# Where the last three up projections stand in a layer's last feed-forward chunk

## The chip, the cores and the metric

The kernel runs on one core of a Trainium2 chip. TensorE (PE in the profile) multiplies matrices, VectorE (DVE) and ScalarE (ACT) do element-wise work, GpSimd (POOL) does a little of it, and SyncE (SP) issues nearly all DMA transfers. The metric is device time in microseconds (us), the median of several runs. The kernel before takes 2103.15 us: median of 3 runs, from 2100.36 to 2106.13.

## The reference

Two encoder layers work on 256 tokens of width 2048, in float32. Only the second half of a layer matters here; the first half (one input projection, two kinds of attention, one output projection) keeps its form.

```python
def depthwise_conv(u, w, bias):
    up = jnp.pad(u, ((0, 0), (1, 1), (0, 0)))
    return up[:, :-2] * w[0] + up[:, 1:-1] * w[1] + up[:, 2:] * w[2] + bias
...
        x = x + o @ w_out[l]
        h2 = rms_norm(x, ln2_g[l])
        u = depthwise_conv(h2 @ w_up[l], conv_w[l], conv_b[l])
        gate, up = u[..., :D_FF], u[..., D_FF:]
        x = x + (jax.nn.silu(gate) * up) @ w_down[l]
```

D_FF is 5632, so `w_up` is 2048 x 11264 and `w_down` 5632 x 2048 in each layer.

## The kernel before

**Two halves of a number.** A float32 operand is split into a high part (`whi`, written by ScalarE in L112) and the rest (`wlo`, written by VectorE in L113). TensorE multiplies high by high, low by high and high by low. All matmuls go through a helper in L98, so TensorE's work has that one line and is told apart by its tiles.

**Quanta and steps.** All weights are cut into pieces of 1 MB (128 x 2048). The list `quanta` holds them in the order of the program; a quantum is one such piece and the matmuls that use it. A step is half of a quantum, or a third of it for a quantum of the seven-product scheme. The main loop goes through the steps: `split_w` splits the weights of the step four ahead (`SPLIT_AHEAD`, five buffers each of `whi` and `wlo`), then come the matmuls of the step itself, then what the dictionary `side` has due there. When a quantum's last step is split, its `raw` buffer (three of them) is free and SP loads the quantum three ahead (`LOAD_AHEAD`, L733). Splits are traced with a priority of 40 instructions ahead of their place (`AHEAD_PRIO`). From this program a list scheduler makes a fixed order of instructions for each engine, by priority and by its own estimate of when each is ready; on the chip each engine runs its own list in order and waits where data are not there.

**Feed-forward.** The 5632 middle columns are 44 blocks of 128, called f. For each f there are two `up` quanta (`q_up`), which together accumulate gate and value in an `mm` tile of PSUM, and then `glu`: ScalarE and VectorE read the tile (L545, L546), VectorE multiplies by the normalising factor (L547), GpSimd copies a border, the convolution is one ScalarE and two VectorE operations for each half (L555, L557), then Silu, product (L561) and split, which gives `gs[f]`. For each pair of f whose products go through the seven-product scheme, `sums_mid` also makes four sums of blocks (L574 to L577).

The 44 blocks are cut into chunks of 8, 8, 8, 8 and 12 (`CHUNKS`). Output columns are four blocks nb of 512. Within a chunk:

- For the first 8 f (`PART`), output blocks 0 and 1 are computed by a scheme of seven products in place of eight, over pairs of f: four `seven` quanta (`q_seven`), each with three parts. Part 1 first has VectorE form sums of the weights in place (L739, 1024 columns, and L740 and L741, 512 each). Six sums stay open in PSUM from seven(0) to the end of seven(3): two halves of an `mm` tile, both `S` tiles, `tr` and `pv`. Then `add_seven` reads them (L617 to L625). What the scheme leaves out is one `plain` quantum (`q_plain`), for one sub-block, added in L654.
- Output blocks 2 and 3 are computed plainly, by `down` quanta (`q_down`, four f each): down(nb, g), g counting groups of four f. A finished block is added to x in L481.
- In the last chunk blocks 0 and 1 have one `down` quantum each, down(0,2) and down(1,2), for the four f outside of the scheme. down(0,2) takes an `mm` tile, down(1,2) `tr` and `pv`.

PSUM has two `mm` tiles in all. In the kernel before, `q_plain` takes one (`cur["dn"]`) and every later down(2, g) and down(3, g) of the chunk goes into it.

**Order in a chunk.** The first four chunks: ups to one f beyond the chunk, plain, then seven(i) and a down in turn. The last chunk: all ups to f = 43, plain, then as L706 to L722 say:

```python
quanta += [seven(0), down(2, 0), seven(1), down(2, 1), seven(2), down(2, 2), seven(3)]
quanta += [down(3, 0), down(0, 2), down(1, 2), down(3, 1), down(3, 2)]
```

**Leaving a layer.** When an output block is complete in the last chunk, `leave_x` (L694) puts its squares and transposes for the next layer (`square_x`, `turn_x`) at a quantum that comes some places later; the pair of numbers is (quanta later, half). In the last layer it stores the block instead, by DMAs on SP (L637). Two loads of the next layer's attention bias (L323) use the buffers in which the last products of `glu` lie.

Of the kernel before, what the change touches and what calls it, by code (L numbers as in the profile page):

```python
# [11 lines left out]
F32 = mybir.dt.float32  # L12
# [6 lines left out]
P = 128  # L19
L = 2  # L20
T = 256
TT = T // P
# [9 lines left out]
NF = FF // P  # L32
FG = 4


CHUNKS = (8, 8, 8, 8, 12)

PART = 8
PAIRS = PART // 2
# [20 lines left out]
def encoder_kernel(  # L60
# [10 lines left out]
    psum = ctx.enter_context(tc.tile_pool(name="psum", bufs=4, space=bass.MemoryType.PSUM))  # L71
# [333 lines left out]
    quanta = []  # L405
# [5 lines left out]
    def two(ps, w_h, w_l, mv, first, last):  # L411

        mm(ps, w_h, mv, first, False)
        mm(ps[:, 1], w_l, mv[:, 0], False, last)
# [12 lines left out]
    cur = {}  # L427
# [99 lines left out]
    def q_up(l, f, u):  # L527
        def body(q, half, hi, lo):
            if u == 0 and half == 0:
                cur["up"] = psum.tile([P, 2, 2, T], F32, name="mm", bufs=2)  # L530
            ps = cur["up"]
            hv, lv = (w.rearrange("p (k j n) -> p k j n", k=4, j=2) for w in (hi, lo))
            for j in range(2):
                for kk in range(4):
                    k = 8 * u + 4 * half + kk
                    two(ps[:, j], hv[:, kk, j], lv[:, kk, j], xs[k], k == 0, k == KD - 1)
            if u == 1 and half == 1:
                glu(l, f, ps)
        return body

    def glu(l, f, ps):
        ux = halo[f % 2]
        r = T // GRID_W
        t = work.tile([P, 2, T], F32, name="prob", bufs=2)
        nc.scalar.activation(t, ps[:, :, 0], AF.Copy)  # L545
        nc.vector.tensor_add(t, t, ps[:, :, 1])  # L546
        nc.vector.tensor_mul(ux[:, :, r:r + T], t, st["r2"][:, None, :].to_broadcast([P, 2, T]))  # L547

        nc.gpsimd.tensor_copy(ux[:, :, 1:r], ux[:, :, T:T + r - 1])  # L549
        nc.gpsimd.tensor_copy(ux[:, :, T + r:T + 2 * r - 1], ux[:, :, r + 1:2 * r])  # L550
        y = work.tile([P, 2, T], F32, name="pT", bufs=4)
        for j in range(2):
            c = j * NF + f
            w0, w1, w2, b = (par["conv"][:, l, i, c:c + 1] for i in range(4))
            nc.scalar.activation(y[:, j, :], ux[:, j, r:r + T], AF.Identity, scale=w1, bias=b)  # L555
            for w, o in ((w0, 0), (w2, 2 * r)):
                nc.vector.scalar_tensor_tensor(y[:, j, :], ux[:, j, o:o + T], w, y[:, j, :],  # L557
                                               op0=ALU.mult, op1=ALU.add)
        nc.scalar.activation(t[:, 0, :], y[:, 0, :], AF.Silu)  # L559
        m = work.tile([P, T], F32, name="bias", bufs=2)  # L560
        nc.vector.tensor_mul(m, t[:, 0, :], y[:, 1, :])  # L561
        gs[f] = middle(l, f)
        split(gs[f][:, 0], gs[f][:, 1], m)
        ms[f] = m
        if f % 2 and f < NF - CHUNKS[-1] + PART:
            sums_mid(l, f // 2, ms.pop(f - 1), ms.pop(f))
# [17 lines left out]
    def q_seven(l, c, i):  # L584

        f = sum(CHUNKS[:c]) + 2 * i
        p = f // 2
        a, b = slice(0, P), slice(P, T)

        def body(q, part, hi, lo):  # L590
            if i == 0 and part == 0:
                t = psum.tile([P, 2, 512], F32, name="mm", bufs=2)
                ps = {1: t[:, 0], 6: t[:, 1]}
                for n, name, k in ((5, "S", 2), (7, "S", 2), (3, "tr", 1), (4, "pv", 1)):
                    ps[n] = psum.tile([P, 512], F32, name=name, bufs=k)
                cur["seven"] = ps
            ps = cur["seven"]
            hv, lv = (w.rearrange("p (k n) -> p k n", k=2) for w in (hi, lo))
            todo = (((3, ss[p, 3]), (1, gs[f][:, :, a])),
                    ((7, ss[p, 2]), (5, ss[p, 0])),  # L600
                    ((4, gs[f + 1][:, :, b]), (6, ss[p, 1])))[part]
            for j, (n, x2) in enumerate(todo):
                for x_part, w in ((0, hv), (1, hv), (0, lv)):
                    mm(ps[n], x2[:, x_part], w[:, j], i == 0 and x_part == 0 and w is hv,
                       i == PAIRS - 1 and w is lv)
            if i == PAIRS - 1 and part == 2:
                with tc.high_priority(offset=AHEAD_PRIO):
                    add_seven(ps)
        return body
# [17 lines left out]
    def leave_x(q, l, nb, after):  # L627

        if l + 1 < L:
            at(q + after[0], square_x, nb, half=after[1])  # L630
            at(q + after[0], turn_x, l + 1, 0, nb, half=after[1])
            if nb == NB - 1:
                at(q + after[0], stat_x, 0)
        else:
            m = slice(nb * 512, (nb + 1) * 512)
            for tt in range(TT):
                nc.sync.dma_start(out=out[:, tt, m], in_=x[:, tt, m])  # L637
# [17 lines left out]
        return body  # L655

    def q_down(l, c, nb, g):
        f0, nf = sum(CHUNKS[:c]), CHUNKS[c]

        def body(q, half, hi, lo):  # L660
            if nb >= 2:
                ps = cur["dn"]
            elif half == 0:

                ps = cur["dn", nb] = (psum.tile([P, TT, 512], F32, name="mm", bufs=2) if nb == 0 else
                                      _Both(*(psum.tile([P, 512], F32, name=n, bufs=1) for n in ("tr", "pv"))))
            else:
                ps = cur["dn", nb]
            hv, lv = (w.rearrange("p (k n) -> p k n", k=2) for w in (hi, lo))
            i = FG * g + 2 * half  # L670

            last = l == L - 1 and c == len(CHUNKS) - 1 and nb == NB - 1
            cut = nf - FG if last or nb < 2 else 0
            if last and i >= cut:
                if i == cut:
                    add_x(nb, ps)
                    cur["end"] = [psum.tile([P, 512], F32, name="S", bufs=2) for _ in range(TT)]
                ps = _Both(*cur["end"])
            three(ps, (gs[f0 + i], gs[f0 + i + 1]), hv, lv, i in (0, cut), i in (cut - 2, nf - 2),
                  last and i == nf - 2)  # L680
            if i < nf - 2:
                return
            if last:
                for tt in range(TT):
                    xv = x[:, tt, nb * 512:(nb + 1) * 512]
                    nc.vector.tensor_add(xv, xv, ps[:, tt])  # L686
                    for j in range(2):
                        m = slice(nb * 512 + j * 256, nb * 512 + (j + 1) * 256)
                        (nc.sync, nc.scalar)[j].dma_start(out=out[:, tt, m], in_=x[:, tt, m])
                return  # L690
            with tc.high_priority(offset=4 * AHEAD_PRIO if c == len(CHUNKS) - 1 and nb == NB - 1 else 0):
                add_x(nb, ps)
            if c == len(CHUNKS) - 1:
                leave_x(q, l, nb, ((2, 0), (1, 1), (6, 0), (1, 1))[nb])  # L694
        return body

    for l in range(L):
        for j in range(NJ):
            for u in range(4):
                quanta.append((a["w_in"][l, j, u], q_win(l, j, u), ""))  # L700
        for grp in "ba":
            for nb in range(NB):
                for u in range(2):
                    quanta.append((a["w_out"][l, 0 if grp == "a" else 1, nb, u], q_wout(l, grp, nb, u), ""))
        f = 0
        for c, nf in enumerate(CHUNKS):  # L706

            end = min(sum(CHUNKS[:c + 1]) + 1, NF)
            while f < end:
                for u in range(2):  # L710
                    quanta.append((a["w_up"][l, f, u], q_up(l, f, u), "up"))
                f += 1
            down = lambda nb, g: (a["w_down"][l, sum(CHUNKS[:c]) // FG + g, nb], q_down(l, c, nb, g), "")
            seven = lambda i: (a["w_seven"][l, c, i], q_seven(l, c, i), "seven")
            quanta.append((a["w_plain"][l, c], q_plain(l, c), ""))
            if nf == 8:
                for i in range(4):
                    quanta += [seven(i), down(2 + i // 2, i % 2)]
            else:
                quanta += [seven(0), down(2, 0), seven(1), down(2, 1), seven(2), down(2, 2), seven(3)]  # L720
                quanta += [down(3, 0), down(0, 2), down(1, 2), down(3, 1), down(3, 2)]


    steps = [(q, h) for q in range(len(quanta)) for h in range(3 if quanta[q][2] == "seven" else 2)]
# [228 lines left out]
```

## Time and profile before

The profile is one execution, with a span (first to last instruction) of 2101.8 us. PE is TensorE matmuls, PEld its weight loads. "Granted clock" is the share of TensorE's full speed that the chip allowed.

| | |
|---|---|
| median of 3 runs | 2103.15 us (2100.36 to 2106.13) |
| the profiled execution's own time | 2103.54 us |
| its span | 2101.8 us |
| mean granted clock | 0.998 |
| TensorE matmuls busy | 2088.1 us |
| VectorE busy | 1724.5 us |
| ScalarE busy | 1221.6 us |
| read from HBM | 404.42 MB, 193 GB/s over the span |

A row of a timeline or of the chain begins with start and length in us. A number in square brackets is the idle time of the engine before the instruction, with what ended it. A row of waits gives the sum in us, the number of waits and the longest. A row of windows gives the stretch, its length, the busy time and count of each engine in turn (PE, PEld, DVE, ACT, POOL), then the granted clock, the share of busy DMA engines, and GB/s. A row of a group gives its count, busy time, mean ns of one, and the idle time before it. A row of loads gives count, size and us from issue to landing.

The last chunk of the first layer ends with its down quanta at about 1005 to 1046 us of the span, that of the second layer at the end of the span.

### The profile page before, as it was taken

The numbers are of one execution on the slowest core, as the hardware profiler recorded it, in microseconds if no ns is written. First come the engines' busy times: TensorE is split into PE (matmuls) and PEld (weight loads), VectorE is DVE, ScalarE is ACT, GpSimd is POOL, SyncE is SP. The second block draws the span as 40 slices with busy tenths as digits, with TensorE's granted clock in tenths as the row PEclk, the third lists the DMA queues.
The fourth block names the chain that finished last, engine by engine and source line by source line (L and its number), as shares of the span: only waits on it lengthen the run. The fifth ranks groups of instructions, "written<-read, shape, count | busy, mean of one in ns | idle before, by whom it ended". The sixth has DMA issues, their size and how long they took to land.

```text
span 2101.8 us, 29190 instructions
## 1 busy us (share of the span) xinstructions
PE 2088.1 (99%) x10816; PEld 1792.2 (85%) x10816; DVE 1724.5 (82%) x2604; ACT 1221.6 (58%) x1817; POOL 167.5 (8%) x237
## 2 busy tenths in 40 slices
PE   9999999999999999999999999999999999999998
PEld 8888888888888888888788888888888888888886
DVE  7786757898998989988857866678989989899886
ACT  7566656565655555556555665566555555565653
POOL 0011100100101001011000011001001010100110
PEclk9999999999999999999999999999999999999999
DMA  9544555556465565655555455555565656546554
GB/s 346 200 152 156 178 180 179 182 211 210 164 239 198 203 203 186 231 188 182 218 182 179 161 171 169 172 180 191 205 208 184 225 196 213 194 179 240 183 191 148
DMA packets 62145, 408.42 MB, mean 194 GB/s; under 512 B 7345, under 2 KB 9905, under 8 KB 13745
## 3 DMA queue, kind: packets, MB, share of 16 engines
q1 hardware_dynamic: 61280, 405.46, 55.9%
q8 instruction: 85, 1.39, 0.3%
q10 hardware_dynamic: 720, 1.08, 0.2%
q14 instruction: 60, 0.48, 0.1%
HBM read 404.42 MB, written 2.10 MB: 193 GB/s over the span
## 4 chain that ended last, share of the span: by engine, by line
PE 99%; DMA 1%; ACT 0%; DVE 0%; issue 0%; ACTq 0%; DVEq 0%
PE mm L98 89%; PE S L98 4%; PE pv L98 3%; PE tr L98 2%; PE tr L373 1%; DMA raw<-in_w_down 1%; PE tr L307 1%; PE S L149 0%; DVE wlo L113 0%; ACT whi L112 0%; ACT qtok L274 0%; ACT kT L315 0%; DVE x L686 0%; ACT tq L618 0%; DVE ones L90 0%
## 5 line engine op out<-in xcount | busy, mean ns | idle before, releaser
L112 ACT ACTIVATE whi<-raw 128x1024 fp32r<-128x1024 f32 (+1 forms) x797 | 829.9, 1057 | 696.9 <-PE mm L98 411.3
L113 DVE TENSOR_TENSOR wlo<-raw,whi 128x1024 fp32r<-128x1024 f32 (+1 forms) x797 | 963.7, 1220 | 278.9 <-ACT whi L112 238.3
L98 PE MATMUL mm<-xs,whi 128*128 128x512 f32 x2816 | 976.7, 390 | 0.0
L98 PE MATMUL mm<-xs,wlo 128*128 128x256 f32 x2816 | 794.1, 282 | 0.0
L98 PEld LDWEIGHTS mm<-xs,whi 128*128 128x128 f32 x2816 | 528.4, 188 | 110.4
L98 PEld LDWEIGHTS mm<-xs,wlo 128*128 128x128 f32 x2816 | 532.2, 189 | 0.9
L98 PE MATMUL mm<-whi,mid 128*128 128x512 f32 x1412 | 371.7, 394 | 7.1 <-ACT whi L112 7.1
L98 PEld LDWEIGHTS mm<-whi,mid 128*128 128x128 f32 x1412 | 265.2, 190 | 62.6 <-ACT whi L112 7.9
L98 PE MATMUL mm<-whi,xs 128*128 128x512 f32 x1152 | 294.3, 393 | 1.4 <-ACT qtok L274 1.3
L98 PEld LDWEIGHTS mm<-whi,xs 128*128 128x128 f32 x1152 | 213.1, 188 | 44.3 <-ACT qtok L274 1.8
L98 PE MATMUL mm<-wlo,mid 128*128 128x512 f32 x706 | 201.4, 392 | 0.0
L98 PE MATMUL mm<-wlo,xs 128*128 128x512 f32 x576 | 159.5, 393 | 0.0
L98 PEld LDWEIGHTS mm<-wlo,mid 128*128 128x128 f32 x706 | 132.1, 188 | 27.0
L557 DVE SCALAR_TENSOR_TENSOR pT<-halo,conv,pT 128x256 f32<-128x256 f32 x352 | 147.6, 478 | 0.9
L549 POOL COPY halo<-halo 128x6 f32<-128x6 f32 x88 | 34.3, 390 | 1199.6 <-DVE halo L547 1199.6
L98 PEld LDWEIGHTS mm<-wlo,xs 128*128 128x128 f32 x576 | 107.3, 188 | 21.6
L555 ACT ACTIVATE pT<-halo,conv 128x256 f32<-128x256 f32 x176 | 95.1, 587 | 5.8 <-DVE halo L547 5.7
L550 POOL COPY halo<-halo 128x6 f32<-128x6 f32 x88 | 79.4, 903 | 0.2 <-POOL halo L549 0.2
L547 DVE TENSOR_TENSOR halo<-prob,acc_b 128x512 f32<-128x512 f32 x88 | 60.6, 689 | 2.1
L546 DVE TENSOR_TENSOR prob<-prob,mm 128x512 f32<-128x512 f32 x88 | 59.8, 680 | 0.0
L559 ACT ACTIVATE prob<-pT 128x256 f32<-128x256 f32 x88 | 35.6, 404 | 35.0 <-DVE pT L557 35.0
L545 ACT ACTIVATE prob<-mm 128x512 f32<-128x512 f32 x88 | 51.4, 584 | 7.4 <-PE mm L98 7.4
(180 smaller groups left out, 1475.9 us busy)
## 6 DMA issues: line engine op xcount, KB each, us to landing
raw<-in_w_up SPq DMA_DIRECT2D x176, 1024.0 KB, 4.9
raw<-in_w_in SPq DMA_DIRECT2D x71, 1024.0 KB, 4.9
raw<-in_w_down SPq DMA_DIRECT2D x48, 1024.0 KB, 4.9
raw<-in_w_seven SPq DMA_DIRECT2D x40, 1024.0 KB, 5.0
raw<-in_w_out SPq DMA_DIRECT2D x32, 1024.0 KB, 4.9
raw<-in_w_plain SPq DMA_DIRECT2D x10, 1024.0 KB, 4.9
bias<-in_bias SPq DMA_DIRECT2D x16, 160.0 KB, 2.5
x<-in_x SPq DMA_DIRECT2D x4, 512.0 KB, 11.0
```

Source lines behind the costliest of these rows:

```text
L98: nc.tensor.matmul(ps, lhsT, rhs, start=start, stop=stop, skip_group_check=True)
L112: high = nc.scalar.activation(hi, src, AF.Copy)
L113: nc.vector.tensor_sub(lo, src, hi.bitcast(F32))
L307: nc.tensor.transpose(ps[:, j, tt * P:(tt + 1) * P], qn[tt][:, p + j, :], ident)
L545: nc.scalar.activation(t, ps[:, :, 0], AF.Copy)
L546: nc.vector.tensor_add(t, t, ps[:, :, 1])
L547: nc.vector.tensor_mul(ux[:, :, r:r + T], t, st["r2"][:, None, :].to_broadcast([P, 2, T]))
L549: nc.gpsimd.tensor_copy(ux[:, :, 1:r], ux[:, :, T:T + r - 1])
L550: nc.gpsimd.tensor_copy(ux[:, :, T + r:T + 2 * r - 1], ux[:, :, r + 1:2 * r])
L555: nc.scalar.activation(y[:, j, :], ux[:, j, r:r + T], AF.Identity, scale=w1, bias=b)
L557: nc.vector.scalar_tensor_tensor(y[:, j, :], ux[:, j, o:o + T], w, y[:, j, :], op0=ALU.mult, op1=ALU.add)
L559: nc.scalar.activation(t[:, 0, :], y[:, 0, :], AF.Silu)
```

## The change

Only the last chunk of each layer is reordered; the lists of the first four chunks come out the same. The ups before the plain quantum now end at f = 40. The two quanta of f = 41, 42 and 43 stand behind seven(0), seven(1) and seven(2). After seven(3) come all eight down quanta: down(2,0), (2,1), (2,2), (0,2), (3,0), (1,2), (3,1), (3,2). In the last chunk, down(2,0) and down(3,0) each take a new `mm` tile in place of the one that `q_plain` took. The due places of blocks 0 and 2 in `leave_x` go from (2, 0) and (6, 0) to (3, 0) and (5, 0).

```diff
     def q_down(l, c, nb, g):
-        f0, nf = sum(CHUNKS[:c]), CHUNKS[c]
+        f0, nf, i0 = sum(CHUNKS[:c]), CHUNKS[c], FG * g
 
         def body(q, half, hi, lo):
             if nb >= 2:
+                if nf > PART and i0 == 0 and half == 0:
+                    cur["dn"] = psum.tile([P, TT, 512], F32, name="mm", bufs=2)
                 ps = cur["dn"]
...
-            i = FG * g + 2 * half
+            i = i0 + 2 * half
...
-                leave_x(q, l, nb, ((2, 0), (1, 1), (6, 0), (1, 1))[nb])
+                leave_x(q, l, nb, ((3, 0), (1, 1), (5, 0), (1, 1))[nb])
...
-            end = min(sum(CHUNKS[:c + 1]) + 1, NF)
+            up = lambda f: [(a["w_up"][l, f, u], q_up(l, f, u), "up") for u in range(2)]
+            down = lambda nb, g: [(a["w_down"][l, sum(CHUNKS[:c]) // FG + g, nb], q_down(l, c, nb, g), "")]
+            seven = lambda i: [(a["w_seven"][l, c, i], q_seven(l, c, i), "seven")]
+
+            end = sum(CHUNKS[:c]) + PART + 1
...
-                quanta += [seven(0), down(2, 0), seven(1), down(2, 1), seven(2), down(2, 2), seven(3)]
-                quanta += [down(3, 0), down(0, 2), down(1, 2), down(3, 1), down(3, 2)]
+
+                for i in range(PAIRS):
+                    quanta += seven(i)
+                    if f < NF:
+                        quanta += up(f)
+                        f += 1
+                for nb, g in ((2, 0), (2, 1), (2, 2), (0, 2), (3, 0), (1, 2), (3, 1), (3, 2)):
+                    quanta += down(nb, g)
```

More of the change, by code (lines that the diff above doesn't have):

```diff
@@ L706, in encoder_kernel @@
         for c, nf in enumerate(CHUNKS):
-            end = min(sum(CHUNKS[:c + 1]) + 1, NF)
+            up = lambda f: [(a["w_up"][l, f, u], q_up(l, f, u), "up") for u in range(2)]
+            down = lambda nb, g: [(a["w_down"][l, sum(CHUNKS[:c]) // FG + g, nb], q_down(l, c, nb, g), "")]
+            seven = lambda i: [(a["w_seven"][l, c, i], q_seven(l, c, i), "seven")]
+            end = sum(CHUNKS[:c]) + PART + 1
             while f < end:
-                for u in range(2):
-                    quanta.append((a["w_up"][l, f, u], q_up(l, f, u), "up"))
+                quanta += up(f)
                 f += 1
-            down = lambda nb, g: (a["w_down"][l, sum(CHUNKS[:c]) // FG + g, nb], q_down(l, c, nb, g), "")
-            seven = lambda i: (a["w_seven"][l, c, i], q_seven(l, c, i), "seven")
             quanta.append((a["w_plain"][l, c], q_plain(l, c), ""))
-            if nf == 8:
-                for i in range(4):
-                    quanta += [seven(i), down(2 + i // 2, i % 2)]
-            else:
-                quanta += [seven(0), down(2, 0), seven(1), down(2, 1), seven(2), down(2, 2), seven(3)]
-                quanta += [down(3, 0), down(0, 2), down(1, 2), down(3, 1), down(3, 2)]
+            if nf == PART:
+                for i in range(PAIRS):
+                    quanta += seven(i) + down(2 + i // 2, i % 2)
+            else:
+                for i in range(PAIRS):
+                    quanta += seven(i)
+                    if f < NF:
+                        quanta += up(f)
+                        f += 1
+                for nb, g in ((2, 0), (2, 1), (2, 2), (0, 2), (3, 0), (1, 2), (3, 1), (3, 2)):
+                    quanta += down(nb, g)
     steps = [(q, h) for q in range(len(quanta)) for h in range(3 if quanta[q][2] == "seven" else 2)]
```

## The prediction

> **What bounds the kernel now.** I read the page first, then the waits of TensorE, the end of the chain, and the timeline around the longest waits.
>
> ```profile
> span 2101.8 us, 29190 instructions
> PE 2088.1 (99%) x10816; PEld 1792.2 (85%) x10816; DVE 1724.5 (82%) x2604; ACT 1221.6 (58%) x1817; POOL 167.5 (8%) x237
> ```
> ```profile
> PE mm L98 <- ACT whi L112: 7.1, 2, 3.7
> PE mm L98 <- ACT qtok L274: 1.3, 2, 0.7
> ```
>
> TensorE (PE) is busy 2088.1 of 2101.8 us. Of the 13.7 us that are left, 7.1 are two waits for a high half of weights (whi), 1.3 are two short ones; the rest is the start and the tail. No matmul is added or removed, so there is nothing to gain but these two waits and what hangs on them. Both lie in the section that the change reorders, one in each layer:
>
> ```profile
> 1022.21 1.07 PE L98 MATMUL mm<-wlo,mid 128*128 128x512 f32 x4
> 1026.61 3.68 PE L98 MATMUL mm<-whi,mid 128*128 128x512 f32 x9 [3.34 <-ACT whi L112]
> ```
> ```profile
> 2073.42 4.21 PE L98 MATMUL mm<-whi,mid 128*128 128x512 f32 x9 [3.74 <-ACT whi L112]
> ```
>
> The reader is to see the number in brackets: TensorE stood 3.34 and 3.74 us. Behind each wait it is also slow for a while. The chain of waits gives the stretches, with their matmuls, and an undisturbed stretch of the same shape to compare:
>
> ```profile
> 1026.61 9.18 PE mm L98 x32
> ...
> 1070.75 53.98 PE mm L98 x238
> ...
> 2073.42 9.95 PE mm L98 x32
> ...
> 2092.44 5.45 PE S L98 x24
> ```
> ```profile
> 1020.00:1030.00 10.00, 6.66 (x24) 5.09 (x23) 8.52 (x11) 3.64 (x5) 0.00 (x0) 0.86 0.98 365
> ```
>
> Undisturbed, a matmul of 512 columns takes 53.98 / 238 = 0.2268 us, so 32 take 7.26. They took 9.18 and 9.95: 1.92 and 2.69 us lost, with a granted clock of 0.86 in the window around the first wait.
>
> Why it waited: each engine runs its instructions in an order fixed when the program is built, so I look at what each engine had in front of it.
>
> ```profile
> 1014.70 1.22 DVE L481 TENSOR_TENSOR x<-x,mm 128x1024 f32<-128x1024 f32 x1 [1.92 <-PE mm L98]
> 1015.84 5.76 DVE L113 TENSOR_TENSOR wlo<-raw,whi 128x1024 fp32r<-128x1024 f32 x5
> ```
> ```profile
> 1017.09 4.87 SPq L733 DMA_DIRECT2D raw<-in_w_down  x3
> ```
> ```profile
> 1022.09 2.01 ACT L112 ACTIVATE whi<-raw 128x1024 fp32r<-128x1024 f32 x2 [4.96 <-DMA raw<-in_w_down]
> 1024.00 0.58 ACT L618 ACTIVATE tq<-mm 128x512 f32<-128x512 f32 x1
> 1025.51 1.06 ACT L112 ACTIVATE whi<-raw 128x1024 fp32r<-128x1024 f32 x1 [0.93 <-DMA raw<-in_w_down]
> ```
> ```profile
> 1025.46 0.68 DVE L619 TENSOR_TENSOR tq<-tq,mm 128x512 f32<-128x512 f32 x1
> ```
>
> VectorE (DVE) waits 1.92 us for the end of down(2,2), then does five splits late; only they free raw buffers, so three loads leave in a bunch from 1017.09, and their data come at 1022.09 and 1025.51. Meanwhile the seven products have just ended. The weights of down(0,2) were split by 1021.6, but its bank is one of the seven's two `mm` halves, read last by L619 at 1025.46. So the fixed order gave TensorE half of down(3,1) first, whose weights came last. Two things fail together: no free bank behind the seven, and late loads.
>
> **The change, part by part.** Counts stay: per layer 44 ups, 20 sevens, 5 plain quanta and 24 downs, with the same splits and 1 MB loads (each issued on SP at its quantum's new place). Only the last chunk moves: seven(0), up 41, seven(1), up 42, seven(2), up 43, seven(3), then eight downs, blocks 2 and 3 in new tiles.
>
> (1) *The wait behind seven(3) goes.* down(2,0), (2,1), (2,2) come next, and their bank is the `mm` tile that up 43 left. down(0,2) comes 3 x 24 x 0.2268 = 16.3 us after the seven's end instead of 5.4. The readout of the seven takes as long in the chunk before, where splits go between its parts:
>
> ```profile
> 856.84 0.69 DVE L617 TENSOR_TENSOR x<-x,mm 128x512 f32<-128x512 f32 x1
> ...
> 858.78 0.68 DVE L619 TENSOR_TENSOR tq<-tq,mm 128x512 f32<-128x512 f32 x1
> ...
> 872.15 0.68 DVE L625 TENSOR_TENSOR x<-x,pv 128x512 f32<-128x512 f32 x1
> ```
>
> L619 is done 2.6 us after L617 starts, L625 16.0 us after. down(0,2) needs the first at 16.3 us, down(1,2) the last (`pv`) two downs later, at 27.2. Gain: 3.34 + 1.92 + 3.74 + 2.69 = 11.69 us. [...]
>
> (2) *Splits between the sevens.* Does VectorE keep up? Durations:
>
> ```profile
> L113 DVE TENSOR_TENSOR wlo<-raw,whi 128x1024 fp32r<-128x1024 f32 x795 | 962.4, 1222 | 278.8 <-ACT whi L112 238.3 <-PE mm L98 31.7 <-ACT mid L115 4.3
> L557 DVE SCALAR_TENSOR_TENSOR pT<-halo,conv,pT 128x256 f32<-128x256 f32 x352 | 147.6, 478 | 0.9
> L547 DVE TENSOR_TENSOR halo<-prob,acc_b 128x512 f32<-128x512 f32 x88 | 60.6, 689 | 2.1
> L546 DVE TENSOR_TENSOR prob<-prob,mm 128x512 f32<-128x512 f32 x88 | 59.8, 680 | 0.0
> L739 DVE TENSOR_TENSOR raw<-raw 128x1024 f32<-128x1024 f32 x40 | 48.8, 1220 | 0.7
> L561 DVE TENSOR_TENSOR bias<-prob,pT 128x256 f32<-128x256 f32 x88 | 36.8, 418 | 1.0 <-ACT prob L559 1.0
> ...
> L741 DVE TENSOR_TENSOR raw<-raw 128x512 f32<-128x512 f32 x40 | 27.6, 690 | 1.1
> L740 DVE TENSOR_TENSOR raw<-raw 128x512 f32<-128x512 f32 x40 | 27.5, 687 | 0.7
> ```
> ```profile
> 882.00:948.00 66.00, 66.00 (x383) 58.52 (x382) 56.44 (x95) 40.46 (x63) 8.09 (x12) 1.00 0.56 192
> ```
> ```profile
> 821.70:859.80 38.10, 38.10 (x169) 31.53 (x169) 37.35 (x45) 22.85 (x28) 1.18 (x2) 1.00 0.60 217
> ```
>
> Splits in a row start 5.76 / 5 = 1.15 us apart. A seven costs VectorE 1.22 + 0.69 + 0.69 + 3 x 1.15 = 6.05 us, a down 2.30, an up pair 4.60 plus its gate, 0.68 + 0.69 + 4 x 0.48 + 0.42 + 0.42 (the low half of the product, taken like L561) = 4.13. TensorE takes 18 x 0.2268 = 4.08 for a seven, 5.44 for a down, and 64 x 66.00 / 383 = 11.03 for an up pair. Seven and down: splits 8.35 against 9.52, 88%; the window 821.7 to 859.8 is this mix, VectorE 98% busy, and TensorE has no idle time. Seven and up pair: splits 10.65 against 15.11, 70%; with the gate 14.78, 98%. So splits, which are put ahead of other work, have more room than in a mix that already runs without a wait. I cost this part at nothing; its cover is 0.33 us a pair, and what slips is the gate, not the splits.
>
> (3) *One bank pair for three ups.* The seven holds the other `mm` tile, so each up (and down(2,0)) waits until ACT L545 and DVE L546 have read the up before, with a seven, 4.08 us, as cover. An up that ended at the first plain matmul shows the time:
>
> ```profile
> 819.46 1.08 PE L98 MATMUL mm<-whi,mid 128*128 128x512 f32 x4
> ```
> ```profile
> 821.03 0.68 DVE L546 TENSOR_TENSOR prob<-prob,mm 128x512 f32<-128x512 f32 x1
> ```
> ```profile
> 951.39 0.68 DVE L546 TENSOR_TENSOR prob<-prob,mm 128x512 f32<-128x512 f32 x1
> ```
> ```profile
> 982.31 1.08 PE L98 MATMUL mm<-whi,mid 128*128 128x512 f32 x4
> ```
>
> 821.71 - 819.46 = 2.25 us in one case. Up 43 ended at 982.31, so up 40 ended three pairs before, at 949.2, and was read by 952.07: 2.9 us. Cover left: 1.2 to 1.8 us. Cost: nothing.
>
> (4) *The last gate.* down(2,2)'s second half needs up 43's product 4.08 + 10.88 + 2.72 = 17.7 us after that up's end. Before VectorE can finish it may lie: its own 4.13, seven splits up to there (8.1), about 4 us of backlog from (2), and the seven's readout, 2 x 1.22 + 6 x 0.68 = 6.5 (L622 and L624 taken like L481, the others like L617). Without the readout 16.2, with all of it 22.7: a wait of 0 to 5.0 us a layer. I take 0, as the rows 856.84 to 872.15 show the readout spread behind splits over 16 us.
>
> (5) *Due times.* The squares and transposes of blocks 0 and 2 are due at q+3 and q+5, which are the first halves of down(3,1) and down(3,2), as before. Nothing.
>
> (6) *SP.* The next layer's two bias loads wait for buffers that the last gates use:
>
> ```profile
> 989.25 6.94 SPq L323 DMA_DIRECT2D bias<-in_bias  x2
> ```
> ```profile
> raw<-in_w_down SPq DMA_DIRECT2D x48, 1024.0 KB, 4.9
> ```
>
> SP can stand some 6 us between them, with raw loads queued behind. Among downs, three buffers mean a load is called about two quanta (10.9 us) before its split and takes 4.9, so 6 us are spare: nothing, or at worst 1 us.
>
> Sum against the profiled execution: 2103.54 - 11.69 = 2091.85 us, of which the span would be 2090.1. The median of the runs, 2103.15, lies 0.39 lower: **2091.5 us**. With the waits gone the next bound is TensorE itself.
>
> **The rivals.**
>
> *A new wait at the last gate (B).* Part 4 goes to the middle, 2.5 us a layer, and the clock costs 1.92 again: 2 x 4.4 = 8.8 back, 2100.3; at its worst, 5.0 + 2.69, 2106.9. For it: VectorE at 98%. Against it: the readout yields.
>
> *The stall only moves (C).* A fixed order that puts a half with late weights first, as now, at another place: 2103. For it: it happened at this very section. Against it: behind seven(3) three downs with a free bank and loads called in their order.
>
> *Hand-over of the one bank pair (D), slower.* If L546 is put behind the seven's three subtractions (1.22 + 0.69 + 0.69 = 2.6 us), reading ends 5.5 us after the up: 1.4 us of wait at each of six hand-overs, 8.5, and with the clock lost each time (6 x 1.92) 20.0: 2100.0 to 2111.5. It is slower than now from 11.69 / 6 = 1.95 us each, clock included. Against it: 2.25 and 2.9 us in the rows, and waits of 0.7 us that stand alone. [...]
>
> **How the numbers follow.** Forecast 0.60, B 0.18, C 0.08, D 0.14. Runs of the kernel lie up to 3.0 us from their median, so the forecast case reaches down to 2089. Up to 2103 lie nearly all of it, most of B (0.16), half of C and a little of D: 0.81. What a measurement tells from no change is 0.3%, 6.3 us. Faster than 2096.8: the forecast and half of B, 0.69. Within: half of B, C, and 0.05 of D, 0.22. Slower than 2109.5: the rest of D, 0.09.
>
> **What would show it.** Right: TensorE's waits for L112 gone, no stretch of 32 matmuls over 7.3 us, clock 1.00 from 940 us to the layer's end, VectorE near 95% between the sevens. B: a wait of matmuls with `qT` on L113 in down(2,2). D: waits on L546 ahead of ups. I am wrong if a fixed order makes TensorE stand where its data are only just due.

## The result, and the profile after

| | before | after |
|---|---|---|
| median | 2103.19 us (4 runs, 2100.36 to 2106.13) | 2092.13 us (4 runs, 2092.00 to 2092.52) |
| ratio | | 0.9948, 95% interval 0.993 to 0.9965 |
| the profiled execution, and its span | 2103.54, 2101.8 us | 2092.00, 2090.2 us |
| granted clock, mean | 0.998 | 1.000 |

The changed kernel is 11.1 us faster. The forecast was 2091.5, in a range of 2089 to 2103. Two executions among all that follow, one of the kernel before (4248.09 us) and one of down31_first (5413.67 us), took more than twice as long as every other and are left out of the comparisons. First the page after, then TensorE's waits:

```profile
span 2090.2 us, 29185 instructions
PE 2083.5 (100%) x10816; PEld 1789.2 (86%) x10816; DVE 1720.5 (82%) x2604; ACT 1222.3 (58%) x1817; POOL 170.3 (8%) x237
```
```profile
PE mm L98 <- ACT qtok L274: 1.3, 2, 0.7
PE pv L98 <- DVE halfpi L94: 1.1, 1, 1.1
```

The row of 7.1 us on L112 is gone and nothing stands in its place. The work is the same, 10816 matmuls. The window over the whole changed section of the first layer (length, then busy us and count of PE, PEld, DVE, ACT and POOL, then the clock):

```profile
940.00:1050.00 110.00, 110.00 (x553) 93.70 (x552) 96.19 (x126) 66.92 (x96) 7.58 (x11) 1.00 0.60 211
```

TensorE is busy for all of 110 us, at full clock. VectorE behind seven(3), which ends at about 1001.4:

```profile
1001.61 0.69 DVE L617 TENSOR_TENSOR x<-x,mm 128x512 f32<-128x512 f32 x1
...
1005.09 0.68 DVE L619 TENSOR_TENSOR tq<-tq,mm 128x512 f32<-128x512 f32 x1
...
1012.81 1.21 DVE L622 TENSOR_TENSOR x<-x,S 128x1024 f32<-128x1024 f32 x1
...
1015.08 0.42 DVE L113 TENSOR_TENSOR qT<-bias,qT 128x256 fp32r<-128x256 f32 x1
...
1017.68 0.68 DVE L625 TENSOR_TENSOR x<-x,pv 128x512 f32<-128x512 f32 x1
...
1021.78 1.22 DVE L481 TENSOR_TENSOR x<-x,mm 128x1024 f32<-128x1024 f32 x1 [2.16 <-PE mm L98]
```

The bank pair of the seven is free at 1005.8 and TensorE first wants it at 1015.2 (below). VectorE still waits for TensorE ahead of L481, 2.16 us where it was 1.92, and here TensorE does not wait for VectorE.

### The profile page after: what moved, and what is told of

Its sections match the earlier page's. It is cut to its first block, busy times and chain, and to the rows that moved or that the text cites. A ratio compares the mean times of both kernels' runs of the same rounds, so it can differ in the third digit from the quotient of the medians.

```text
span 2090.2 us, 29185 instructions
## 1 busy us (share of the span) xinstructions
PE 2083.5 (100%) x10816; PEld 1789.2 (86%) x10816; DVE 1720.5 (82%) x2604; ACT 1222.3 (58%) x1817; POOL 170.3 (8%) x237
## 4 chain that ended last, share of the span: by engine, by line
PE 99%; DMA 0%; ACT 0%; DVE 0%; issue 0%
PE mm L98 90%; PE S L98 4%; PE pv L98 3%; PE tr L98 2%; PE tr L373 1%; PE tr L307 1%; PE S L149 1%; DMA head<-in_head 0%; ACT qtok L274 0%; ACT kT L315 0%; ACT xs L115 0%; DVE x L688 0%; ACT whi L112 0%
## 5 line engine op out<-in xcount | busy, mean ns | idle before, releaser
L112 ACT ACTIVATE whi<-raw 128x1024 fp32r<-128x1024 f32 (+1 forms) x797 | 830.9, 1057 | 689.9 <-PE mm L98 411.9
L113 DVE TENSOR_TENSOR wlo<-raw,whi 128x1024 fp32r<-128x1024 f32 (+1 forms) x797 | 963.9, 1220 | 270.3 <-ACT whi L112 231.8
L546 DVE TENSOR_TENSOR prob<-prob,mm 128x512 f32<-128x512 f32 x88 | 59.8, 679 | 0.0
```

Of the source, the lines that this page charges most:

```text
L112: high = nc.scalar.activation(hi, src, AF.Copy)
L113: nc.vector.tensor_sub(lo, src, hi.bitcast(F32))
```

## Experiments: which half of the change does it

The change has two halves: the downs come last, and three ups stand between the sevens. Three kernels keep the first and take the second back: no up between the sevens, then two, then one. The paragraphs set off are what was expected before each run; a ratio is to the kernel before, measured beside it, with its 95% interval.

**No up between the sevens (downs_last_only).** Changed kernel, with

```diff
-            end = sum(CHUNKS[:c]) + PART + 1
+            end = min(sum(CHUNKS[:c + 1]) + 1, NF)
```

> Half of the change: the eight downs come last, but all ups stand ahead and the four sevens follow each other directly. My theory (behind seven(3) there was neither a free bank nor weights in time; the downs of blocks 2 and 3 behind it are the cure): the wait behind seven(3) is gone, but VectorE needs 4 x 6.05 = 24.2 us for sevens that TensorE does in 16.3, so TensorE waits 1 to 3 us a layer among the sevens, with some clock lost: 2094 to 2099. Rival (the cure is the ups between the sevens, which relieve VectorE): waits of 5 us and more a layer, 2103 or later.

Measured 2106.68 us, 1.0014 of before (1.0005 to 1.0023): slower than before. The wait behind seven(3) is gone, and the rest of my number failed. TensorE's waits, and the window over the sevens:

```profile
PE S L98 <- ACT whi L112: 3.6, 4, 1.4
PE pv L98 <- ACT whi L112: 3.1, 6, 1.0
PE S L98 <- DVE wlo L113: 1.1, 2, 0.6
```
```profile
984.00:1006.00 22.00, 18.38 (x69) 13.22 (x68) 20.83 (x27) 10.31 (x14) 1.17 (x2) 0.92 0.46 159
```

VectorE is 95% busy and TensorE only 18.38 of 22 us, at a clock of 0.92. The waits come to 3.9 us a layer, where I had 1 to 3, and the lost clock comes on top: over both layers the run is 14.6 us above the changed kernel, 7.3 a layer, so 3.4 a layer more than these waits. I had counted the splits against TensorE's 16.3 us, and left out that up 43's gate (4.1 us of VectorE) falls into the same stretch.

**Two ups between (two_sevens), and one (three_sevens).** Changed kernel, with seven(2) and seven(3) as neighbours:

```diff
-            end = sum(CHUNKS[:c]) + PART + 1
+            end = sum(CHUNKS[:c]) + PART + 1 + (nf > PART)
...
-                    if f < NF:
+                    for _ in range((1, 1, 0, 0)[i]):
```

> The changed kernel with up 41 ahead of the plain quantum, up 42 behind seven(0), up 43 behind seven(1), and seven(2) and seven(3) next to each other. Three neighbouring pairs of sevens cost 14.6 us in the run with the sevens in a row. If every pair costs the same: 2092.1 + 4.9 = 2097. If the four steps that splits run ahead carry one pair (VectorE falls 6.05 - 4.08 = 2.0 us behind in it): 2092 to 2093.

Measured 2092.50 us, 0.9947 (0.9929 to 0.9965), with no wait of TensorE on a split. With `2 * (nf > PART)` and `(1, 0, 0, 0)`, three sevens stand in a row:

> The changed kernel with ups 41 and 42 ahead of the plain quantum, up 43 behind seven(0), and seven(1), (2), (3) next to each other. One neighbouring pair cost 0.4 us, three cost 14.6. If VectorE's lack adds up by 2 us a pair until the lead of four steps is gone: two pairs 1 to 5 us, 2093 to 2097. If every pair after the first costs a third of the 14.6 or more: 2097 to 2099.

Measured 2099.69 us, 0.9985 (0.9975 to 0.9994), beyond both ranges. Its waits are in the last of the three sevens:

```profile
PE S L98 <- ACT whi L112: 3.8, 2, 1.9
PE pv L98 <- ACT whi L112: 0.9, 2, 0.5
```

So with none, one, two and three pairs of sevens next to each other the time is 2092.1, 2092.5, 2099.7 and 2106.7 us. One pair costs next to nothing; from the second pair on each costs 7 us for both layers, lost clock included. That it is the lead of four steps that carries the first pair fits these times, but no run changed that lead. The ups between are needed once the downs have left that place. The other half alone, ups between the sevens with the downs where they were, was not run, nor were the new tiles by themselves.

## Experiments: what was late behind seven(3)

The prediction said that two things failed together there, the bank and the loads. Four edits of the kernel *before* take them apart.

**Weights in the order that TensorE wants (down31_first).**

```diff
-                quanta += [down(3, 0), down(0, 2), down(1, 2), down(3, 1), down(3, 2)]
+                quanta += [down(3, 0), down(3, 1), down(0, 2), down(1, 2), down(3, 2)]
...
-                leave_x(q, l, nb, ((2, 0), (1, 1), (6, 0), (1, 1))[nb])
+                leave_x(q, l, nb, ((1, 1), (1, 1), (6, 0), (1, 1))[nb])
```

> The kernel before with down(3,1) traced, and so loaded, ahead of down(0,2) and down(1,2); ups and sevens as before. My theory: TensorE gets the weights that its fixed order wants first, and down(0,2) needs its bank 10.9 us after the seven: no wait on L112, 2092 to 2094. Rival (VectorE is too full between sevens without the ups): the wait stays at 3 to 4 us a layer, 2101 to 2105.

Measured 2097.14 us (seven runs, 2096.91 to 2101.16), 0.9972 (0.9962 to 0.9983): in neither range. The wait behind seven(3) is gone, as I expected; but blocks 0 and 1 are now complete one quantum later, and TensorE waits at the start of the next layer for the normalised x:

```profile
PE mm L98 <- ACT xs L115: 2.4, 3, 1.7
PE S L149 <- DVE xs L116: 1.9, 2, 1.4
```

**Only TensorE's order (d02_forced).** Here down(3,1)'s first half is held behind down(0,2), whose weights were there. `st["mm"]` is the last matmul that the helper issued.

```diff
-        nc.tensor.matmul(ps, lhsT, rhs, start=start, stop=stop, skip_group_check=True)
+        st["mm"] = nc.tensor.matmul(ps, lhsT, rhs, start=start, stop=stop, skip_group_check=True)
...
+            held = c == len(CHUNKS) - 1 and nb == 3 and i == FG
+            with tc.issue_after(st["d02"].ins) if held else ExitStack():
                 three(ps, (gs[f0 + i], gs[f0 + i + 1]), hv, lv, i in (0, cut), i in (cut - 2, nf - 2),
                       last and i == nf - 2)
+            if nb == 0:
+                st["d02"] = st["mm"]
```

> The kernel before with the matmuls of down(3,1) held behind those of down(0,2) on TensorE, whose weights were split in time. If the seven's bank was just as late as the weights (L619 ended 2.9 us after down(3,0)): TensorE waits 2.5 to 3.3 us for the readout at the same place, 2101 to 2105. If only the late load mattered: no wait, 2092 to 2094.

Measured 2103.18 us, 0.9996 (0.9986 to 1.0005). The first range holds, and the releaser changes its name:

```profile
PE mm L98 <- DVE tq L619: 6.4, 2, 3.6
```
```profile
1026.06 0.80 PE L98 MATMUL mm<-whi,mid 128*128 128x512 f32 x1 [2.86 <-DVE tq L619]
```

The bank was nearly as late as the weights: TensorE starts at 1026.06, where it started at 1026.61. In the profile before, this wait was put down to ScalarE's L112 and a DMA, because the fixed order wanted the late weights first.

**VectorE's wait for L481 out of the way of the split (late_add).** `lows` keeps the VectorE half of each step's split.

```diff
+            held = c == len(CHUNKS) - 1 and nb == 2
+            with tc.issue_after(lows[steps.index((q, 1)) + 3].ins) if held else ExitStack():
+                with tc.high_priority(offset=4 * AHEAD_PRIO if c == len(CHUNKS) - 1 and nb == NB - 1 else 0):
+                    add_x(nb, ps)
-            with tc.high_priority(offset=4 * AHEAD_PRIO if c == len(CHUNKS) - 1 and nb == NB - 1 else 0):
-                add_x(nb, ps)
...
+            lows[s] = st["lo"]
```

> The kernel before with VectorE's add of block 2 (L481) queued behind the split of seven(3)'s last part, so that this split no longer stands behind 1.92 us of waiting for TensorE. If that wait is what made the loads late: the load of down(1,2) leaves 2 us earlier, that of down(3,1) about 1, TensorE's wait shrinks from 3.3 to 2.4 us or less, 2097 to 2101. If VectorE's queue as a whole is late and not this wait: unchanged, 2102 to 2104.

Measured 2092.00 us, 0.9943 (0.9928 to 0.9958): better than either range, and all of the change's gain from one instruction's place. I had counted only the loads. VectorE's timeline shows why:

```profile
1011.62 2.52 DVE L113 TENSOR_TENSOR wlo<-raw,whi 128x1024 fp32r<-128x1024 f32 x2
1014.76 1.22 DVE L481 TENSOR_TENSOR x<-x,mm 128x1024 f32<-128x1024 f32 x1 [0.62 <-PE mm L98]
1015.90 2.35 DVE L113 TENSOR_TENSOR wlo<-raw,whi 128x1024 fp32r<-128x1024 f32 x2
1018.17 0.68 DVE L617 TENSOR_TENSOR x<-x,mm 128x512 f32<-128x512 f32 x1
1018.76 2.35 DVE L113 TENSOR_TENSOR wlo<-raw,whi 128x1024 fp32r<-128x1024 f32 x2
1021.04 0.68 DVE L619 TENSOR_TENSOR tq<-tq,mm 128x512 f32<-128x512 f32 x1
```

L617 now stands in front of two of the splits that preceded it, and L619 ends at 1021.7, not at 1026.1. TensorE's fixed order also changes: down(0,2) now stands ahead of down(3,1). So this run frees bank and loads at once and can't say which counts.

**The bank without the loads (bank_first).** In the kernel before, the splits of down(1,2), which waited for their load, stand in front of L619 on VectorE:

```profile
1021.52 0.68 DVE L617 TENSOR_TENSOR x<-x,mm 128x512 f32<-128x512 f32 x1
1023.18 2.36 DVE L113 TENSOR_TENSOR wlo<-raw,whi 128x1024 fp32r<-128x1024 f32 x2 [0.99 <-ACT whi L112]
```

On ScalarE their high halves stand in front of L618 in the same way (the rows 1022.09 and 1024.00 of the prediction), although L617 reads the same bank from 1021.52 on. Here VectorE's wait of 1.92 us and the late loads stay, and these splits are queued behind the readout on both engines. `st["hold"]` is set to 2 where the last chunk's readout is traced.

```diff
-        nc.scalar.activation(t, ps[1], AF.Copy)
-        nc.vector.tensor_add(t, t, ps[6])
+        st["b618"] = nc.scalar.activation(t, ps[1], AF.Copy)
+        st["b619"] = nc.vector.tensor_add(t, t, ps[6])
...
-            with tc.high_priority(offset=AHEAD_PRIO if s >= KD // 2 else 0):
+            held = st.get("hold", 0)
+            st["hold"] = max(held - 1, 0)
+            with (tc.high_priority(offset=AHEAD_PRIO if s >= KD // 2 else 0),
+                  tc.issue_after(st["b618"].ins) if held else ExitStack(),
+                  tc.issue_after(st["b619"].ins) if held else ExitStack()):
```

> The kernel before; VectorE still waits 1.92 us ahead of L481 and the loads still leave as late, but the splits of down(1,2) are queued behind L618 and L619, so that the seven's first bank pair is free about 2.7 us sooner, and the scheduler now puts down(0,2) ahead of down(3,1) on TensorE. If the late bank is what decides: TensorE waits 0.2 to 0.7 us a layer, 2092.5 to 2094. If the late loads decide: 3 us and more as before, 2101 to 2105.

Measured 2093.31 us, 0.9954 (0.9938 to 0.9971), in the range of the bank. Its VectorE, and TensorE at the place (the added line moves the lines by one: L620 is the L619 of before):

```profile
1014.86 1.22 DVE L481 TENSOR_TENSOR x<-x,mm 128x1024 f32<-128x1024 f32 x1 [1.92 <-PE mm L98]
1016.00 5.76 DVE L113 TENSOR_TENSOR wlo<-raw,whi 128x1024 fp32r<-128x1024 f32 x5
1021.68 0.68 DVE L618 TENSOR_TENSOR x<-x,mm 128x512 f32<-128x512 f32 x1
1023.03 0.69 DVE L620 TENSOR_TENSOR tq<-tq,mm 128x512 f32<-128x512 f32 x1 [0.67 <-ACT tq L619]
```
```profile
1023.77 0.50 PE L98 MATMUL mm<-whi,mid 128*128 128x512 f32 x1 [0.33 <-DVE tq L620]
```

The first two lines are those of the kernel before, to the hundredth in their lengths; only the readout comes at once and not behind a split that waits for its DMA. The three loads leave at 1017.25 to 1021.79, where they left at 1017.09 to 1021.63, and TensorE waits 0.33 us. So the late loads by themselves cost nothing in this order: they mattered because splits that waited for one held up the readout of the bank behind them on ScalarE and VectorE, and because the fixed order had put the later weights first. That the scheduler chose that order because it expected the bank late is my reading: the order changed in both runs that free the bank sooner. An early bank under the old order was not run.

## Experiments: the rivals of the prediction

**The hand-over of one bank pair (D; ups_in_a_row).** Changed kernel with two ups in a row; two_sevens is its comparison, as seven(2) and seven(3) are neighbours in both.

```diff
-                    if f < NF:
+                    for _ in range((2, 1, 0, 0)[i]):
```

> The changed kernel with up 41 and up 42 directly behind each other while the seven holds the other mm tile, up 43 behind seven(1), and seven(2) and seven(3) next to each other (the run above is the comparison for these). If the hand-over of the one bank pair costs what it takes in the changed kernel, 3.0 us from an up's last matmul to the end of L546: TensorE stands 3 us a layer, and with the clock lost 0 to 3.4: 6 to 13 us later than the run above. If the fixed order fills the hand-over with other matmuls: no difference.

Measured 2097.17 us, 0.9968 (0.9956 to 0.998), 4.7 us above two_sevens. Neither range: the scheduler pulls seven(1)'s first part into the hand-over, and it comes before its weights are split.

```profile
968.11 0.73 PE L98 MATMUL tr<-whi,mid 128*128 128x512 f32 x2 [1.08 <-ACT whi L112]
```

It costs 2.3 us a layer, and the granted clock stayed 1.0. Of the waits in both layers 2.2 us are for this split and 0.3 for L546. In the changed kernel the hand-over is covered, but thinly. TensorE at the end of up 41, and VectorE's reading of its tile:

```profile
966.93 0.62 PE L98 MATMUL tr<-whi,mid 128*128 128x512 f32 x2
```
```profile
969.31 0.68 DVE L546 TENSOR_TENSOR prob<-prob,mm 128x512 f32<-128x512 f32 x1
```

It is read 969.99 - 966.93 = 3.06 us after that up, with 4.08 us of seven(1) before the next.

**The last gate (B).** In the changed kernel up 43 ends where seven(3) begins on TensorE:

```profile
997.32 0.62 PE L98 MATMUL tr<-whi,mid 128*128 128x512 f32 x2
```

Its product is whole at 1015.50 (the row of L113 with `qT` in the profile after), 18.2 us later, where I had 17.7 as the time when it is wanted. TensorE did not wait. The scheduler had swapped two halves there; TensorE's timeline before and behind the swap:

```profile
1015.01 0.39 PE L98 MATMUL mm<-whi,qT 128*128 128x512 f32 x1
1015.24 0.39 PE L98 MATMUL mm<-whi,mid 128*128 128x512 f32 x1
...
1017.96 2.88 PE L98 MATMUL mm<-whi,qT 128*128 128x512 f32 x12
```

The alternation of `mid` and `qT` from 1015.24 on is down(0,2)'s first half, in front of the rest of down(2,2)'s second half (all `qT`). The next run (order_kept) undoes that:

```diff
+            with tc.issue_after(st["held"].ins) if nf > PART and nb == 0 else ExitStack():
                 three(ps, (gs[f0 + i], gs[f0 + i + 1]), hv, lv, i in (0, cut), i in (cut - 2, nf - 2),
                       last and i == nf - 2)
+            if nf > PART and nb == 2:
+                st["held"] = st["mm"]
```

> The changed kernel with down(0,2)'s matmuls held behind those of down(2,2) on TensorE, which undoes a swap that the scheduler made there. Up 43's product was whole 18.1 us after that up, and down(2,2)'s second half now starts at 17.7, with its low half first read some 0.9 later: no wait, 2092.0 to 2092.6. If the swap carried the last gate: 2094 or later.

Measured 2092.02 us, 0.9945 (0.9929 to 0.996): no wait, so the swap was not needed. By the order of `three`, a step reads low halves of products only from its fifth matmul on, 0.9 us after its first (4 x 0.2268, an estimate from the undisturbed rate). The run after that (gate_early) asks what the cover is worth. It puts down(0,2) in second place, with down(2,1) held behind it in the same manner, and `leave_x` keeps its due quanta:

```diff
-                leave_x(q, l, nb, ((3, 0), (1, 1), (5, 0), (1, 1))[nb])
+                leave_x(q, l, nb, ((5, 0), (1, 1), (4, 0), (1, 1))[nb])
...
-                for nb, g in ((2, 0), (2, 1), (2, 2), (0, 2), (3, 0), (1, 2), (3, 1), (3, 2)):
+                for nb, g in ((2, 0), (0, 2), (2, 1), (2, 2), (3, 0), (1, 2), (3, 1), (3, 2)):
```

> The changed kernel with down(0,2) in second place behind seven(3), and down(2,1) held behind it on TensorE, so that up 43's product is wanted 12.2 us after that up and not 17.7. If it is ready 18.1 us after the up, as in the changed kernel: TensorE waits about 5 us a layer and loses up to 3.4 of clock, 2102 to 2109. If the splits and the readout of the seven, which stood before it on VectorE, give way: waits of 1 to 2 us, 2094 to 2098.

Measured 2103.95 us, 1.0004 (0.9995 to 1.0014). All of the gain is gone again:

```profile
PE mm L98 <- ACT qT L112: 7.4, 2, 4.0
```
```profile
1013.44 2.08 PE L98 MATMUL mm<-whi,qT 128*128 128x512 f32 x4 [3.44 <-ACT qT L112]
```

TensorE waits here for the high half of the product, which ScalarE finishes 16.0 us after the up; I had reckoned with the whole product. Of the 11.8 us over the changed kernel these waits are 7.4, so some 2 us a layer are left, where I had put up to 3.4 of clock; 3.4 is what downs_last_only took beyond its waits.

## Why the prediction was right, point by point

- **The gain.** In the profiled executions 11.54 us came of 11.69 forecast, and both terms are there: the waits of 3.34 and 3.74 us are gone, and TensorE's busy time fell by 4.6 us (2088.1 to 2083.5), where the slow stretches were put at 1.92 + 2.69 = 4.61.
- **The cause.** "Two things fail together" put the late loads beside the bank, where they worked through it. With the bank early and down(0,2) in front, the wait is 0.33 us with the loads as late as ever (bank_first); with down(0,2) in front and the bank late it is 2.86 us on L619 (d02_forced). The late load held up the readout that stood behind it. The point that the prediction called the cure, three downs with a free bank behind seven(3), holds: TensorE wants the bank 13.8 us after the seven's end (1015.24 - 1001.4; forecast was 16.3, before the swap told above), 9.5 us after it is free.
- **VectorE between the sevens**, costed at nothing: right. It is 96% busy over the section from 951 to 1018 us, and TensorE has no idle time:

```profile
951.00:1018.00 67.00, 67.00 (x343) 57.36 (x342) 64.43 (x84) 41.91 (x54) 5.72 (x8) 1.00 0.64 225
```

  But the prediction gave the ups between no part in the gain, and they have one: without them the same order of downs takes 2106.7 us. That is 7.3 us a layer against the changed kernel, 3.9 of them waits for splits.
- **Hand-over:** 3.06 us, where the rows before gave 2.25 and 2.9; the cover left is 1.0 us. Rival D did not come. With two ups in a row the place costs 2.3 us a layer, though most of that wait is for a split, so D's own price is not shown.
- **Last gate:** ready 18.2 us after up 43, between the bounds of 16.2 and 22.7. The value of 0 was luck in part. The prediction took it because the readout of the seven would yield, but six of its eight VectorE operations, up to L622, came before the product was whole, and by its own 17.7 us TensorE would have waited 0.5. What spared it, by the order of `three`, is that the low half is read 0.9 us into the step, which was not in its working; order_kept, without the swap, has no wait. gate_early, which wants the product 12.2 us after the up, brings 11.8 us back. Rival B was closer than its chance of 0.18 suggests.
- **SP:** the second bias load left at 1015.52, between two loads of weights at 1012.58 and 1017.79, and held up neither: the second left as the split before it ended (1017.77).
- **Rival C**, a stall that only moves, did come in down31_first, where blocks 0 and 1 were finished later; not in the change, whose due places are the old ones.

No version beat the changed kernel: late_add (2092.00) and order_kept (2092.02) reach the same time, in which TensorE is busy for 2083.5 of 2090.2 us (the changed kernel).

## What to carry to other kernels

When an engine that is busy everywhere else waits at one place, ask what stands in front of the releaser in its own queue: here a readout that frees a bank stood behind a split that waited for a DMA (that readout ended at 1026.1 us, and at 1023.7 in bank_first), and the profile named the DMA. Here the wait was cured by more independent work behind the seven, and also by the place of one instruction; both gave the same 2092 us. Work that is moved away to make that cover may itself have been cover: the downs could leave the sevens only because the ups took their place (2092.1 us with them there, 2106.7 without).

## What the hardware showed unexpectedly

**The kernel before varies with its clock.** In one comparison 23 runs of it took 2098.75 to 2106.49 us, and the slower ones had the lower mean granted clock: 1.0 in the fastest, 0.999 or 0.998 in those from 2100.86 to 2104.33, 0.997 in all from 2104.67 on. Where the mean clock reads 1.0, 2098.75 is 6.6 us above the changed kernel, about the two waits' 7.1; the rest of the gain, up to 7.7 us in a run, goes with the clock. That the waits themselves are the same in every run is inferred: a trace of the kernel before was kept for one execution only. The changed kernel's own runs lie within 0.5 us.

**The clock fell to half after 1.6 to 3.3 us of idle time.** In the profile before, around each wait:

```profile
1023.30:1026.60 3.30, 0.00 (x0) 0.00 (x0) 2.84 (x4) 2.34 (x3) 0.00 (x0) 1.00 0.99 358
1027.30:1030.60 3.30, 3.30 (x10) 2.52 (x9) 3.26 (x5) 0.69 (x1) 0.00 (x0) 0.50 0.74 296
2069.70:2071.70 2.00, 0.00 (x0) 0.00 (x0) 0.75 (x1) 1.84 (x2) 0.00 (x0) 1.00 1.00 406
2071.80:2078.50 6.70, 5.08 (x12) 4.01 (x13) 6.63 (x9) 2.63 (x4) 0.00 (x0) 0.50 0.25 106
```

In the first layer it fell about when TensorE resumed and stayed at 0.50 for one stretch of 3.3 us; in the second it fell 2 us into the wait and stayed for twice as long. With the sevens in a row (downs_last_only), waits of 0.55 and 1.04 us in 3.4 us came ahead of a clock of 0.51; in down31_first nearly the same share of idle time, with waits of 1.66 and 1.44 us, left it at 1.00:

```profile
991.40:994.80 3.40, 1.80 (x7) 0.92 (x6) 2.53 (x4) 1.82 (x2) 0.00 (x0) 1.00 0.00 0
994.80:998.20 3.40, 3.40 (x10) 2.60 (x9) 3.37 (x5) 0.68 (x3) 0.00 (x0) 0.51 0.56 157
```
```profile
1045.00:1048.60 3.60, 1.94 (x13) 1.35 (x10) 3.60 (x6) 3.40 (x8) 0.00 (x0) 1.00 0.59 246
1048.60:1052.00 3.40, 1.96 (x10) 1.43 (x11) 3.12 (x6) 1.78 (x6) 0.17 (x1) 1.00 0.94 308
```

TensorE was busy 1.80 of 3.40 us ahead of the fall, and 1.94 of 3.60 and 1.96 of 3.40 without one. These rows do not show what decides between the two.
